# Dilated attention stage: sums read back at a written place, gate and first O loaded behind the last transposing transfer, the last pair's q scaled on VectorE

## The chip, the cores and the metric

The kernel runs on one core of a Trainium2 chip. The metric is device time in microseconds. A core has engines that each work through their own instructions in order: TensorE (PE, with PEld for its weight loads), VectorE (DVE), ScalarE (ACT), GpSimd (POOL) and SyncE (SP). SP issues most of the transfers, ACT some; the issues stand in the engine's order, so a transfer that must wait holds those behind it. Transfers issued by SP and ACT share eight semaphores in turn: an issue also waits until the transfer eight issues before it, on the same semaphore, has landed.

## The reference

Two layers on one sequence of 1024 positions, width 1024. Layer 0 uses latent attention, layer 1 dilated window attention; each layer ends with a squared-ReLU MLP. The change lies in layer 1's mixer:

```python
DIL_GROUPS = ((128, 1), (512, 4), (2048, 16))      # (window, dilation)

def dilated_mixer(h, pos, w_in, g_q, g_k, rel_bias, w_o):
    B, S, _ = h.shape
    proj = (h @ w_in).reshape(B, S, N_DIL_GROUPS, 3, DIL_HEADS, DIL_HEAD_DIM)
    outs, lses = [], []
    for gi, (window, dilation) in enumerate(DIL_GROUPS):
        q = rms_norm(proj[:, :, gi, 0], g_q[gi])
        k = rms_norm(proj[:, :, gi, 1], g_k[gi])
        v = proj[:, :, gi, 2]
        table = rel_bias[:, gi * DIL_HEADS:(gi + 1) * DIL_HEADS]
        o, lse = dilated_group(q, k, v, pos, table, window, dilation)
        outs.append(o)
        lses.append(lse)
    o_all = jnp.stack(outs, axis=0)
    wts = jax.nn.softmax(jnp.stack(lses, axis=0), axis=0)
    o = jnp.einsum('gbsh,gbshd->bshd', wts.astype(o_all.dtype), o_all)
    return o.reshape(B, S, DIL_HEADS * DIL_HEAD_DIM) @ w_o
```

`dilated_group` is softmax attention over the keys within the window, at multiples of the dilation, with a bias per head. Three groups of 16 heads of 64 are merged with weights from their softmax denominators, and the result goes through `w_o`.

## The kernel before, in words

The dilated stage (`dil`, from about 1535 to 2330 us) walks over 3 groups x 8 head pairs x 4 steps, in that order. Each step takes a quarter of the 1024 rows of one head pair: PE projects q and k in two halves of 24 matmuls (`psproj`), VectorE and GpSimd normalise them, PE transposes the rows into `kT` (`psq`, L2316), forms the scores of earlier rows (`pss`, L2345), and multiplies older probabilities with v (`psav`, L2424 and L2425). Numbers are split into a high and a low half-precision part (`ph` for probabilities, `kT`, `oT`), so a product takes three matmuls. In this half-precision form (`self.half` true) the kernel's normal run is made; a second form of the whole program stands behind a flag and does not run here.

`qkstep` ends with q and k scaled by their norms on VectorE (`qn`, L2305); q then takes its gain on GpSimd (L2307). `attend` makes the scores: VectorE adds the bias and takes the maximum (L2366), ACT exponentiates (`dnb` L2370, `pd` L2372), `ph` is split on ACT (L2409) and GpSimd or VectorE (L2410), and SP transposes it by a transfer, `pT<-ph` (L2411). For the steps after the last projection the transposition is made on PE instead (`pspt`, L2398).

Maxima and sums of all heads are kept in `stat`. Groups 0 and 1 hold their rows in another order than group 2, so what they leave goes through memory: each pair's output `U` (L2448, L2452), and, when the last pair of the group is done, the sums `S0` and `S1` (L2456, L2460). In group 2, `um` (issued by ACT) brings U of groups 0 and 1 back. `finish` of the first pair of group 2 reads the sums back (L2467), four transfers. `factors` turns them into merging weights on VectorE (`mgm` … `mgf`), and `merge` multiplies (`um` on GpSimd and U on VectorE, L2501; sums L2503) into one result per pair, which is transposed (`psot`) to O (`oT`) and, for pairs 0 to 5, put into memory (`oTd`).

The output projection behind the stage reads O back by `reload` (L1372, three double pairs of 512 rows, two transfers each) and multiplies with `wo` (`psy`); the raw weights come by the L538 transfers named `wor`. Its gate is a row of the conditioning broadcast to all partitions (L381, 512 KB). These loads are issued by `tail` in the last steps (`wor`, gate) and when the last step, `n == end`, has been issued (first O).

The order on SP, VectorE, ACT and GpSimd is decided by a scheduler from dependencies, priorities by program place, and a simulated timeline. PE's order is pinned as written up to `n == end` (`pin_from`), and scheduled after that. `pinned` keeps an instruction at its written place.

## Time and profile before

| what | value |
|---|---|
| median of 3 runs | 3006.09 us (3002.42 to 3009.18) |
| the profiled execution's own time | 3005.26 us |
| its span | 3003.1 us |
| mean granted PE clock | .985 |
| PE's longest waits of the dilated stage | 6.2, 5.8 and 4.4 us |

The span is what the profile covers; the times of the runs hold a little more. A row of the timeline gives start, duration, engine, line, operation, tiles written and read, and in brackets the idle time before it with what ended it. A row of the waits gives the total, the count and the longest wait in us.

### The profile page before, as it was taken

The page shows a single profiled execution, that of the slowest core. Times are in us where ns is not written, and L with a number is a line of the kernel's source. Part 1 is how long each engine was busy: PE and PEld are TensorE (multiplying, and loading weights), DVE is VectorE, ACT ScalarE, POOL GpSimd, SP SyncE. Part 2 cuts the span into 40 slices and gives each one's busy share as a digit, 9 for nine tenths or more (in the row PEclk, how much of TensorE's full clock was granted, in tenths as well). Part 3 has the DMA queues.
Part 4 walks back from the last instruction along what each step waited for, and adds up shares of the span by engine and source line. Part 5 has one row for each costly group of instructions (what it writes and reads, how often), then busy time and mean ns, then how long its engine had stood idle before and what let it go on. Part 6 is the DMA issues. An engine that isn't in the chain of part 4 may idle for free. (4 is left out here: it accounts for less than half of the span.)

```text
span 3003.1 us, 54490 instructions
## 1 busy us (share of the span) xinstructions
PE 2827.4 (94%) x20148; PEld 1676.0 (56%) x20148; DVE 2251.4 (75%) x4902; ACT 1684.2 (56%) x3491; POOL 922.6 (31%) x1276
## 2 busy tenths in 40 slices
PE   6878999999999999999999989998998989999998
PEld 5634566544444444444468878876875434444443
DVE  5687777658988966788768877776886699779565
ACT  4677888825455534533238777775664355555341
POOL 6578888700211000000123344453552002110010
PEclk9999999999999999999999999999999999999999
DMA  6267455425654799546436666565656555457763
GB/s 209 72 169 161 94 117 101 131 84 188 235 188 168 251 278 289 199 159 225 171 116 148 146 139 165 145 128 117 150 129 171 144 191 210 158 186 248 238 196 86
DMA packets 589680, 503.08 MB, mean 168 GB/s; under 512 B 292277, under 2 KB 482018, under 8 KB 589402
## 3 DMA queue, kind: packets, MB, share of 16 engines
q1 hardware_dynamic: 553722, 400.74, 47.9%
q0 software_dynamic: 25248, 87.22, 7.9%
q10 hardware_dynamic: 10432, 11.54, 1.6%
q8 instruction: 159, 2.61, 0.4%
q14 instruction: 119, 0.97, 0.1%
HBM read 317.40 MB, written 125.12 MB: 147 GB/s over the span
## 5 line engine op out<-in xcount | busy, mean ns | idle before, releaser
L534 PE MATMUL psm<-hf,wf 128*128 128x512 f16 x896 | 335.8, 381 | 11.1 <-DVE wf L161 11.1
L532 PE MATMUL psm<-hf,wf 128*128 128x512 f16 x896 | 341.0, 381 | 5.0 <-ACT wf L156 5.0
L533 PE MATMUL psm<-d,d 128*128 128x512 f16 x896 | 340.8, 381 | 4.7 <-DVE d L161 4.7
L534 PE MATMUL psm<-d,d 128*128 128x512 f16 x896 | 340.7, 380 | 0.0
L533 PE MATMUL psm<-hf,wf 128*128 128x512 f16 x896 | 340.6, 380 | 0.0
L532 PE MATMUL psm<-d,d 128*128 128x512 f16 x896 | 335.0, 380 | 0.3 <-ACT d L156 0.3
L1276 POOL TENSOR_TENSOR pp<-p,pp 128x1024 f16<-128x1024 f32 x125 | 275.4, 2209 | 57.9 <-ACT pp L1269 47.8
L532 PE MATMUL psproj<-wqk,hTp 128*128 128x256 f16 x1024 | 283.0, 276 | 0.0
L533 PE MATMUL psproj<-wqk,hTp 128*128 128x256 f16 x1024 | 282.3, 276 | 0.0
L534 PE MATMUL psproj<-wqk,hTp 128*128 128x256 f16 x1024 | 282.0, 275 | 0.0
L156 ACT ACTIVATE d<-ufr 128x1024 f16<-128x1024 f32 x112 | 117.8, 1052 | 211.3 <-PE psm L534 173.3
L897 DVE TENSOR_REDUCE mx<-pmx 128x1 f32<-128x512 f32 x240 | 162.8, 687 | 78.8 <-PE pmx L895 77.4
L161 DVE SCALAR_TENSOR_TENSOR d<-ufr,d 128x1024 f16<-128x1024 f32 x112 | 136.5, 1219 | 76.5 <-ACT d L156 76.4
L1268 ACT ACTIVATE p<-pss 128x512 f32<-128x512 f32 x256 | 149.9, 590 | 43.2 <-PE pss L1259 41.8
L2372 ACT ACTIVATE pd<-pd,dnb 128x192 f32<-128x192 f32 (+2 forms) x384 | 167.3, 437 | 4.1 <-POOL y L2301 2.3
L534 PEld LDWEIGHTS <-wf 128*128 128x128 f16 x896 | 87.8, 98 | 123.3 <-DVE wf L161 19.2
L532 PEld LDWEIGHTS <-wf 128*128 128x128 f16 x896 | 87.9, 98 | 112.9 <-ACT wf L156 10.9
L534 PEld LDWEIGHTS <-d 128*128 128x128 f16 x896 | 87.9, 98 | 111.0 <-issue 6.4
L532 PEld LDWEIGHTS <-d 128*128 128x128 f16 x896 | 88.0, 98 | 106.3 <-issue 2.2
L533 PEld LDWEIGHTS <-d 128*128 128x128 f16 x896 | 87.9, 98 | 106.4 <-issue 2.5
L2410 POOL TENSOR_TENSOR ph<-pd,ph 128x512 f16<-128x512 f32 (+1 forms) x121 | 113.3, 942 | 109.3 <-ACT ph L2409 109.1
L533 PEld LDWEIGHTS <-wf 128*128 128x128 f16 x896 | 88.0, 98 | 104.9 <-issue 1.8
(439 smaller groups left out, 8122.2 us busy)
## 6 DMA issues: line engine op xcount, KB each, us to landing
ufr<-uf SPq DMA_DIRECT2D x112, 512.0 KB
w2r<-in_mlp_w SPq DMA_DIRECT2D x96, 512.0 KB
adaw<-in_ada_w SPq DMA_DIRECT2D x80, 512.0 KB
w1r<-in_mlp_w SPq DMA_DIRECT2D x64, 512.0 KB
wqkr<-in_dil_w_in SPq DMA_DIRECT2D x96, 256.0 KB
wvr<-in_dil_w_in SPq DMA_DIRECT2D x34, 512.0 KB
uf<-ub POOLq DMA_DIRECT2D x32, 512.0 KB, 3.8
uf<-ua POOLq DMA_DIRECT2D x32, 512.0 KB, 3.3
```

The source lines that it names most:

```text
L156: nc.scalar.activation(hi, src, AF.Copy, scale=scale)
L161: return nc.vector.scalar_tensor_tensor(lo, src, scale, hi, op0=ALU.mult, op1=ALU.subtract, accum_out=self.seen[:, self.nseen - 1 : self.n ...
L532: mm(out, lh, rh, start=first, stop=False)
L533: mm(out, lh, rl, start=False, stop=False)
L534: mm(out, ll, rh, start=False, stop=last)
L897: nc.vector.tensor_reduce(maxes[h][:, 2 * j + b : 2 * j + b + 1], ps, op=ALU.max, axis=AX.X)
L1268: nc.scalar.activation(p[:, b * 512 : (b + 1) * 512], ps[b], AF.Exp, scale=1.0 / self.ss)
L1276: eng.tensor_tensor(q[:, 1], p, q[:, 0], op=ALU.subtract)
L2372: nc.scalar.activation(p[:, e, lo:hi], p[:, e, lo:hi], AF.Exp, scale=1.0 / self.ss, bias=nb[:, e : e + 1], accum_out=stat[:, g, t, 1, 2 * ...
L2410: (nc.gpsimd if i or u["g"] == 2 else nc.vector).tensor_tensor(lo, p, hi, op=ALU.subtract)
```

## The change

Four edits, all within the half-precision form. First, the read-back of the sums becomes a function, `sums_back(k)`, with pinned transfers: `S0` is read back when pair 2 of group 1 is finished, and `S1` when pair 0 of group 2 is, the place in the code where both were read before. Second, the gate's load leaves `tail` and becomes a callback, `back`. Third, `back` and the first O loads are issued one step later, when step `end + 1` has been written out. Fourth, the gain of q for the last pair of group 2 is multiplied on VectorE.

```diff
     def dil(self, at0, at1, tail, wqk, vd, back=None):
...
-            nc.gpsimd.tensor_tensor(qq, qq, gain[:, g : g + 1, :].unsqueeze(1).broadcast_to([P, 2, 2, 64]), op=ALU.mult)
+            (nc.vector if self.half and (g, u["pr"]) == (2, 7) else nc.gpsimd).tensor_tensor(qq, qq, gain[:, g : g + 1, :].unsqueeze(1).broadcast_to([P, 2, 2, 64]), op=ALU.mult)
...
+                if (g, pr) == (1, 2):
+                    sums_back(0)
                 return
 
             if pr == 0:
-                for k in range(2):
-                    v = Sd[k].rearrange("(l t r) e -> r l t e", t=8, r=2)
-                    for i in range(2):
-                        nc.sync.dma_start(out=stat[64 * i : 64 * i + 64, k].rearrange("p t k h -> p t (k h)"), in_=v[i])
+                sums_back(1)
...
+        def sums_back(k):
+
+            v = Sd[k].rearrange("(l t r) e -> r l t e", t=8, r=2)
+            for i in range(2):
+                self.pinned(nc.sync.dma_start(out=stat[64 * i : 64 * i + 64, k].rearrange("p t k h -> p t (k h)"), in_=v[i]))
...
-                    for pp in range(3):
-                        self.reload(O, src, pp, 0, nc.sync)
+                    if not self.half:
+                        for pp in range(3):
+                            self.reload(O, src, pp, 0, nc.sync)
+            if self.half and n == end + 1:
+                back()
+                for pp in range(3):
+                    self.reload(O, src, pp, 0, nc.sync)
...
+        def back():
+            got["gate"] = k.gate(1, 0)
+
...
             if tp == 3:
-                got["gate"] = k.gate(1, 0)
+                if not half:
+                    back()
```

On SP, where the sums of group 1 have just been written (`S`), before:

```order
L2460 DMA S_16274<-stat 512x1x32
L2467 DMA stat<-S_16274 64x8x32 x2
L2452 DMA U<-U_24430 512x1x128
L2411 DMA_TRANSPOSE pT_25491<-ph_25490 128x16x128
L2411 DMA_TRANSPOSE pT_25646<-ph_25645 128x8x128
L1968 DMA wqkr_25803<-in_dil_w_in 128x4x128
L2452 DMA U<-U_24430 512x1x128
```

and the same place now (weights of the projection are `wqkr`, the bias is `bt`):

```order
L2460 DMA S_16274<-stat 512x1x32
L2452 DMA U<-U_24432 512x1x128
L2411 DMA_TRANSPOSE pT_25493<-ph_25492 128x16x128
L2411 DMA_TRANSPOSE pT_25648<-ph_25647 128x8x128
L1968 DMA wqkr_25805<-in_dil_w_in 128x4x128
L2452 DMA U<-U_24432 512x1x128
L1968 DMA wqkr_25805<-in_dil_w_in 128x4x128
L2411 DMA_TRANSPOSE pT_25785<-ph_25784 128x8x128
L2354 DMA bt_26745<-bias_139 128x2x128
L2411 DMA_TRANSPOSE pT_25912<-ph_25911 128x8x128
L1968 DMA wqkr_26070<-in_dil_w_in 128x4x128
L2479 DMA stat<-S_16274 64x8x32 x2
```

The two read-backs have gone from right behind the write of `S` to behind four more transposes, and stand between two weight loads.

On SP at the end of the stage, before:

```order
L538 DMA wor_29204<-in_dil_w_o 128x2x512
L381 DMA gate_29465<-gates 128x1024
L538 DMA wor_29467<-in_dil_w_o 128x2x512
L2411 DMA_TRANSPOSE pT_29128<-ph_29127 128x8x128
L538 DMA wor_29472<-in_dil_w_o 128x2x512
L1372 DMA oT_29536<-oTd 128x2x512 x2
L1372 DMA oT_29539<-oTd 128x2x512 x2
L1372 DMA oT_29542<-oTd 128x2x512
L2411 DMA_TRANSPOSE pT_29252<-ph_29251 128x8x128
L1372 DMA oT_29542<-oTd 128x2x512
L2411 DMA_TRANSPOSE pT_29383<-ph_29382 128x8x128
L1372 DMA oT_29786<-oTd 128x2x512 x2
```

and now:

```order
L538 DMA wor_29204<-in_dil_w_o 128x2x512
L538 DMA wor_29465<-in_dil_w_o 128x2x512
L2411 DMA_TRANSPOSE pT_29128<-ph_29127 128x8x128
L538 DMA wor_29470<-in_dil_w_o 128x2x512
L2411 DMA_TRANSPOSE pT_29252<-ph_29251 128x8x128
L2411 DMA_TRANSPOSE pT_29383<-ph_29382 128x8x128
L381 DMA gate_29607<-gates 128x1024
L1372 DMA oT_29609<-oTd 128x2x512 x2
L1372 DMA oT_29612<-oTd 128x2x512 x2
L1372 DMA oT_29615<-oTd 128x2x512 x2
L1372 DMA oT_29786<-oTd 128x2x512 x2
```

The last three transposes now stand ahead of the gate and all of O.

On PE behind the last projection, from the last matmul of the scores on, before:

```order
L2345 MATMUL pss_29546<-kT_28967 128x256
L532 LDWEIGHTS oT_29536
L532 MATMUL psy_29849<-wo_29334,oT_29536 128x512
L533 LDWEIGHTS oT_29536
L533 MATMUL psy_29849<-wo_29334,oT_29536 128x512
L534 LDWEIGHTS oT_29536
```

and now:

```order
L2345 MATMUL pss_29535<-kT_28967 128x256
L2398 MATMUL pspt_29549<-ident,pd_29550 128x128
L2316 MATMUL psq_29570<-ident,qn_29365 128x128 x4
L2525 MATMUL psot_29581<-ident,U_28418 128x128 x4
L2525 MATMUL psot_29588<-ident,U_28418 128x128 x4
L2398 MATMUL pspt_29549<-ident,pd_29550 128x128
L2398 MATMUL pspt_29549<-ident,pd_29559 128x128 x2
```

Before, 22 `psy` matmuls of the output projection stood between these scores and the first `pspt`. Now the transpositions follow directly, and the first `psy` comes behind the next scores.

## The prediction

> **What bounds the kernel now.** I read the page first, then PE's waits in the dilated stage, then three of those waits up their queues.

> ```profile
> PE 2827.4 (94%) x20148; PEld 1676.0 (56%) x20148; DVE 2251.4 (75%) x4902; ACT 1684.2 (56%) x3491; POOL 922.6 (31%) x1276
> PE psav L2424 <- DMA pT<-ph: 21.0, 9, 6.2
> PE psq L2316 <- POOL qn L2307: 5.8, 1, 5.8
> ```

> PE is busy 94% of the span, so the change is worth only the PE idle time that it removes, and what follows from it. The last two rows are those of PE's waits from 1770 to 2420 us (total, count, longest) that the diff touches. Three single waits are longer than 4 us, and each has a second price:

> ```profile
> 2060.00:2080.00 20.00, 13.77 (x117) 11.13 (x115) 7.00 (x28) 8.02 (x31) 5.61 (x12) 0.83 0.73 161
> 2260.00:2280.00 20.00, 14.84 (x143) 12.12 (x141) 10.91 (x39) 11.78 (x36) 4.69 (x8) 0.94 1.10 262
> 2280.00:2300.00 20.00, 13.67 (x90) 8.98 (x89) 15.29 (x39) 5.35 (x19) 9.66 (x18) 0.81 0.62 153
> 2070.38 0.29 PE L2424 MATMUL psav<-vs,pT 128*128 128x128 f16 x1 [6.23 <-DMA pT<-ph]
> 2073.56 0.42 PE L534 MATMUL psproj<-wqk,hTp 128*128 128x256 f16 x1
> 2076.35 0.27 PE L533 MATMUL psproj<-wqk,hTp 128*128 128x256 f16 x1
> ```

> In the windows the numbers are the busy time of PE, PEld, DVE, ACT and POOL, then the granted clock, the DMA share and GB/s. PE loses most, and the clock falls to .83, .94 and .81, in just the windows with the long waits. After the 6.23 us wait a projection matmul lasts .42 us until 2276, then .27 again: about 2.6 us of the next step go to the half clock. Short waits (2.94 us, below) show no such fall. [...]

> **Sums of group 1 read back (stall A).**

> ```profile
> 2056.32 0.56 SPq L2460 DMA_DIRECT2D S<-stat  x1
> 2062.71 1.21 SPq L2467 DMA_DIRECT2D stat<-S  x2
> 2064.01 0.58 SPq L2452 DMA_DIRECT2D U<-U  x1
> 2064.70 4.93 SPq L2411 DMA_TRANSPOSE pT<-ph  x2
> SPq L2467 <- DMA S<-stat: 5.7, 1, 5.7
> 2057.77 1.58 POOL L2410 TENSOR_TENSOR ph<-pd,ph 128x256 f16<-128x256 f32 x2 [1.01 <-ACT ph L2409]
> 2058.11 0.75 DVE L2432 TENSOR_REDUCE U<-psav 128x128 f32<-128x256 f32 x2
> ```

> SP works strictly in order. It stands 5.7 us until the sums written at 2056.32 have landed, then issues two read-backs, the write of U, and only then the transpose whose `ph` was complete at 2059.35 (2057.77 + 1.58). PE wanted that transpose at 2070.38 − 6.23 = 2064.15. Without the read-backs the U write goes out when its reduce is done, 2058.86 (2058.11 + .75). From the U issue to `psav` it was 2070.38 − 2064.01 = 6.37 us; kept, `psav` starts at 2065.2, or 1.1 us late. The rings were still busy with loads issued just before, so I add .7: 1.8 remains of 6.23. Gone: 4.4 us and the half clock behind it, 2.65: **7.1 us** (6.2 if 2.7 us remain; 8.9 if nothing does).

> The read-backs now stand two transposes later, ahead of a weight load; their two issues (1.21 us) fall in SP's free time, and the factors on VectorE (`mgm`) that need them stand later in its order too, behind the next steps' q work. I cost that at nothing; if a factor waits there for the read, the q work queued behind it on VectorE waits, and PE with it, one for one.

> **Sums of group 0 (stall A').**

> ```profile
> SPq L2467 <- DMA S<-stat: 2.2, 1, 2.2
> 1807.39 1.93 SPq L2411 DMA_TRANSPOSE pT<-ph  x1
> 1811.62 0.23 PE L2424 MATMUL psav<-vs,pT 128*128 128x128 f16 x1 [2.94 <-DMA pT<-ph]
> 1870.85 0.23 PE L2424 MATMUL psav<-vs,pT 128*128 128x128 f16 x1 [1.26 <-DMA pT<-ph]
> ```

> The same pattern, 2.94 us. The transpose could be issued 2.8 us earlier (2.2 waited, and one of two issues in 1.21), but it stands behind the same loads of v as its sister of the next pair of pairs, which still left 1.26 us at 1870.85. I take 1.6 left, so **1.3 us** gained (bounds 0 and 2.9). The new place, behind the U write of pair 2, costs two issues, 1.1 us, which the next transposes have in hand.

> **Gate and first O (stall B), q of the last pair (stall C).**

> ```profile
> SPq L381 <- DMA um<-U: 4.4, 1, 4.4
> 2264.66 0.34 SPq L381 DMA_DIRECT2D gate<-gates  x1
> 2266.64 0.37 SPq L538 DMA_DIRECT2D wor<-in_dil_w_o  x1
> 2268.69 1.84 SPq L2411 DMA_TRANSPOSE pT<-ph  x1
> 2277.57 0.29 PE L2424 MATMUL psav<-vs,pT 128*128 128x128 f16 x1 [4.36 <-DMA pT<-ph]
> 2289.82 0.69 PE L2316 MATMUL psq<-ident,qn 128*128 128x128 f32 x2 [5.83 <-POOL qn L2307]
> 2285.97 2.49 POOL L2501 TENSOR_TENSOR um<-um,mgf 128x512 f32<-128x512 f32 x2
> 2282.75 0.68 DVE L2305 TENSOR_TENSOR qn<-psproj,dry 128x512 f32<-128x512 f32 x1
> 2283.35 1.15 DVE L2501 TENSOR_TENSOR U<-U,mgf 128x512 f32<-128x512 f32 x1
> 2296.65 0.68 DVE L2501 TENSOR_TENSOR U<-U,mgf 128x512 f32<-128x512 f32 x1
> ```

> B: the gate load waited 4.4 us for its DMA slot. In the new order a `wor` load takes that slot and its wait, so only the gate's own issue, one slot, and its 512 KB ahead of the transpose go. The transpose moves up to the second `wor`'s place, 2266.64 against 2268.69, 2.1 us, and its packets pass the gate's: I estimate 3.3 us, `psav` at 2274.3. It then wants kT, which ACT makes behind a weight conversion that now stands earlier; I put the end of this projection half at 2279.4.

> C: `qn` is ready on VectorE at 2283.43 (2282.75 + .68), but GpSimd scales it only after four `um` products, the last two of which end at 2288.46, and PE's 5.83 us are spent on that. On VectorE the scaling stands behind one product U·mgf: .68 us alone, 1.15 beside a busy GpSimd. The scaling of 128x256 elements has no VectorE row: .35 (half of the .68 of a 128x512 one) to 1.3 (a GpSimd product's length, if it must wait one out); I take .5, nearest to the .68 row. [...]

> With B's advance `qn` is done at about 2280.8 and `psq` starts at 2282.6 instead of 2289.82: PE still waits 3.2 us there. Now to what is next:

> ```profile
> 2295.45 0.83 PE L2345 MATMUL pss<-kT 64*128 64x256 f16 x12
> 2296.21 0.39 PE L532 MATMUL psy<-wo,oT 128*128 128x512 f16 x1
> 2300.75 0.38 PE L532 MATMUL psy<-wo,oT 128*128 128x512 f16 x1
> 2296.06 0.68 DVE L2296 TENSOR_REDUCE dms<-dsq 128x8 f32<-128x512 f32 x1
> 2300.25 0.28 DVE L2366 CUSTOM_DVE_ANT_0 pd<-pss,bt 128x128 f32<-128x128 f32 x1
> 2301.94 1.48 PE L2398 MATMUL pspt<-ident,pd 128*128 128x128 f32 x4 [0.81 <-ACT pd L2372]
> 2323.03 0.33 PE L2398 MATMUL pspt<-ident,pd 128*128 128x128 f32 x1 [1.74 <-ACT pd L2372]
> ```

> The scores end at 2296.21, and `pspt` can start only at 2301.94, since VectorE works through `dms` … `qn` from 2296.06 before it reaches them at 2300.25. Before, 22 `psy` matmuls (2296.21 to 2300.75) fill that gap. They need the first O. With its loads behind the last transpose, the order puts all `psy` behind `pspt`, `psq`, `psot` and the next scores: the 5.7 us become PE idle time, some 6.5 with two scalings (.5 each) more on VectorE.

> Sum for the end: from `psq` to the end of these scores it was 6.4 us, an estimated 2.2 of them by the half clock; 4.2 kept, they end at 2286.8 instead of 2296.21, 9.4 us earlier; then 6.5 us idle, `pspt` at about 2293.3. Before, at 2301.94, 22 `psy` of .216 us were done, which is the same as having been there at 2297.2: 3.9 us gained, less about 1.3 for a half clock behind the new idle time and a wait for kT, plus 1.74 − .7, since the third chain at 2323.03 gets more cover and the second less. **3.6 us** (−3 to +9).

> Total 7.1 + 1.3 + 3.6 = 12.0. The profiled execution took 3005.26 (span 3003.1), .83 under the median 3006.09; from the median I forecast 2994.1. About 6 us (0.2%) is what a measurement here can tell from no change.

> **Rivals.**

> *All stalls vanish.* The transposes land in time and the uncovered chain runs without its VectorE queue: 8.9 + 2.9 + 9 = 20.8, so 2985. For it: the queue's 5.7 us are the plain cause of A. Against: 1.26 us is left at 1870.85, and `dms` to scores is plain work.

> *The uncovered chain eats the end, and A keeps half.* The half clock stays on from the 3.2 us wait through the 6.5 us one, which costs about 2.6 us for a projection half and 1.5 for the rest: the end is −1. The transposes still stand behind the loads, A gives 5 and A' 0: together 4, so 3002.

> *The moves do nothing.* If U's write, not the read-back, holds the transpose, A stays: only 4.9 us, 3001. It shares its chance with the last.

> *Slower: the first O comes late.* Its loads stand behind the last transpose, which waits for GpSimd's `ph` behind four `um` products.

> ```profile
> 2290.42 1.23 SPq L2411 DMA_TRANSPOSE pT<-ph  x1
> 2291.75 3.09 SPq L1372 DMA_DIRECT2D oT<-oTd  x6
> SPq L538 <- DMA um<-U: 13.6, 1, 13.6
> ```

> Before, that transpose left at 2290.42. The `um` products can start with the factors, near 2280.2; four of 1.25 and two of `ph` put it near 2287.5, the loads to 2293, the first pair landed near 2296, before `psy` wants it at 2298. Each us later costs one. It decides from 2310: no gain; 2316 is 0.2% slower. Possible if an O load inherits the slot that held the `wor` loads for 13.6 us behind a read of U; in the new order only the last load of the second half does, and its matmuls come after 2330. With the issue at 2316 and some 2 us to land, the end would be 8 us later than before: 3014.

> **How the numbers follow.** Forecast .53 (2988 to 2999), all vanish .10, chain or nothing .29, slower .08. The range takes in the first three: 2985 to 3003.5. Faster by over 0.2%: the first two and a little of the third, .67; within 0.2% .25; slower .08.

> **What will show it.** Right, if `psav` near 2065 waits under 3 us with the clock at 1.00 from 2060 to 2080; if `psq` near 2283 waits about 3 us on VectorE; if `pspt` afterwards waits 5 to 7 us for ACT. Wrong, if `psav` still waits for SP, if `mgm` waits for the read-backs, or if `psy` waits for a DMA of O.

## The result and the profile after

| | before | change |
|---|---|---|
| median of 8 runs | 3004.49 us | 2995.98 us |
| lowest to highest | 3002.42 to 3010.56 | 2991.36 to 2998.11 |
| profiled execution, its span | 3005.26, 3003.1 | 2996.41, 2994.6 |
| mean granted clock of the span | .985 | .983 |

The ratio of the change to before is .9966, with a 95% interval of .9955 to .9977. That is about 10 us by the ratio and 8.5 by the medians. The forecast was 2994.1, a gain of 12.0 from 3006.09. The total came out as forecast, but the profile shows that it is not made of the forecast's terms.

PE's waits of the changed kernel from 1770 to 2420 us come first (total, count, longest):

```profile
PE psav L2424 <- DMA pT<-ph: 11.2, 7, 4.1
PE pss L2345 <- DVE qn L2305: 5.8, 1, 5.8
PE psot L2525 <- DVE U L2508: 4.3, 2, 2.3
```

The waits for transposed probabilities went from 21.0 us to 11.2, and the 5.8 us of `psq` for GpSimd's q have become .50 for VectorE's (below). Two rows are new: `pss` on `qn` (5.8) and `psot` on the merged U (4.3). Next, four windows of the same kernel (busy time of PE, PEld, DVE, ACT and POOL, then the granted clock):

```profile
2050.00:2070.00 20.00, 18.28 (x194) 15.72 (x192) 13.11 (x48) 14.49 (x54) 8.65 (x17) 1.00 1.12 222
2085.00:2105.00 20.00, 15.66 (x131) 12.74 (x128) 16.15 (x49) 10.63 (x37) 12.73 (x18) 0.83 0.49 107
2260.00:2280.00 20.00, 14.47 (x114) 10.63 (x115) 14.68 (x44) 11.48 (x36) 7.30 (x9) 0.83 0.70 166
2280.00:2300.00 20.00, 11.23 (x88) 8.72 (x86) 16.72 (x54) 7.06 (x23) 5.05 (x11) 0.74 0.63 198
```

and single PE instructions of it, with the idle time before them and its releaser in brackets:

```profile
1812.25 0.22 PE L2424 MATMUL psav<-vs,pT 128*128 128x128 f16 x1
2062.94 0.23 PE L2424 MATMUL psav<-vs,pT 128*128 128x128 f16 x1 [1.09 <-DMA pT<-ph]
2093.28 0.63 PE L2525 MATMUL psot<-ident,U 128*128 128x128 f32 x4 [2.28 <-DVE U L2508]
2095.96 1.09 PE L2525 MATMUL psot<-ident,U 128*128 128x128 f32 x4 [2.06 <-DVE U L2508]
2270.51 0.23 PE L2424 MATMUL psav<-vs,pT 128*128 128x128 f16 x1 [3.12 <-DMA pT<-ph]
2279.59 0.44 PE L2316 MATMUL psq<-ident,qn 128*128 128x128 f32 x2 [0.50 <-DVE qn L2307]
2288.99 1.46 PE L2345 MATMUL pss<-kT 64*128 64x256 f16 x11 [5.80 <-DVE qn L2305]
2291.98 0.48 PE L2398 MATMUL pspt<-ident,pd 128*128 128x128 f32 x1 [1.53 <-ACT pd L2372]
```

Stall A (6.23 us) is down to 1.09 and stall A' (2.94) is gone. The dip of the clock at 2070 is gone too, but a new dip to .83 stands at 2085 to 2105, with the two `psot` waits, and a deeper one (.74) at 2280 to 2300, with the 5.80 and 1.53 us. At 2260 to 2280 the clock was .94 before and is .83 now: behind the shorter `psav` wait (3.12 us against 4.36) the half clock lasts 6.83 us against 3.41.

Where the 8.5 us of span went is read from the starts of the same matmuls in both traces. The tile views give the last ones; each row ends with the first and last start and the form. Before:

```profile
L2425 PE MATMUL psav<-vs,pT x640: 192/193/261, 1564.8 to 2327.7; 128*128 128x64 f16 x160
L534 PE MATMUL psy<-wo,oT x256: 377/379/380, 597.9 to 2395.0; 128*128 128x512 f16 x128
L534 PE MATMUL psm<-d,d x896: 377/379/634, 992.7 to 2992.2; 128*128 128x512 f16 x180
```

and of the change:

```profile
L2425 PE MATMUL psav<-vs,pT x640: 192/193/261, 1564.7 to 2322.5; 128*128 128x64 f16 x160
L534 PE MATMUL psy<-wo,oT x256: 377/379/390, 598.8 to 2390.6; 128*128 128x512 f16 x128
L534 PE MATMUL psm<-d,d x896: 377/379/631, 992.3 to 2983.7; 128*128 128x512 f16 x180
```

The lead is 5.2 us at the end of the stage's `psav`, 4.4 at the end of the output projection and 8.5 at the last MLP matmul. So **half of the lead arises behind everything that the change touches**: the MLP takes 597.2 us before (2992.2 − 2395.0) and 593.1 now. The same subtraction, for stretches between numbered matmuls, gives a table for all kernels that were run. Each entry is that kernel's stretch minus the stretch of before, in one profiled execution of each:

| kernel | start to ~1788 | to ~2050 (A') | to ~2190 (A) | to ~2264 | to last `psav` (end) | to last `psy` | MLP |
|---|---|---|---|---|---|---|---|
| change | +2.3 | −4.6 | −3.8 | 0 | +.9 | +.8 | −4.1 |
| change again | +.7 | −2.6 | −2.4 | +1.7 | +2.9 | +.8 | −4.1 |
| s1_mid | +1.3 | −3.8 | −4.8 | 0 | +.1 | +.8 | −4.1 |
| undo_sums | +1.6 | +2.6 | −.5 | 0 | +.3 | +.8 | −4.1 |
| s0_only | +5.0 | −3.9 | −.7 | 0 | +2.3 | +.8 | −4.1 |
| undo_q | −.5 | −4.0 | −2.3 | +1.7 | +6.9 | +.8 | −4.1 |
| gate_o | +2.6 | +1.0 | −1.0 | 0 | +5.4 | +.8 | −4.1 |
| q_only | +1.3 | +1.5 | −.4 | 0 | −1.3 | −.6 | −.4 |
| sums_q | +3.3 | −2.0 | −3.4 | +1.7 | +1.6 | 0 | −.5 |
| mid_sums_q | +1.0 | −.3 | −2.4 | +1.7 | −.9 | −.6 | −.5 |
| o_early | +2.1 | −2.2 | −4.2 | 0 | −1.2 | +.1 | −4.1 |
| mid_o_early | +1.1 | −2.9 | −4.1 | 0 | −1.9 | −.6 | −1.7 |
| wor_late_p | +2.7 | −2.2 | −3.9 | +1.7 | −10.9 | −.1 | −1.7 |

The first column stands ahead of everything that the edits move, so it says how far single executions wander: −.5 to +5.0. The 0 or +1.7 of the column to 2264 is the same kind of thing, one half clock more or less. The last column hardly wanders; it takes one of three values.

### The profile page after: what moved, and what is told of

It is laid out like the page before. It is cut to its first block, busy times and chain, and to the rows that moved or that the text cites. A ratio compares the mean times of both kernels' runs of the same rounds, so it can differ in the third digit from the quotient of the medians.

```text
span 2994.6 us, 54486 instructions
## 1 busy us (share of the span) xinstructions
PE 2829.0 (94%) x20148; PEld 1679.2 (56%) x20148; DVE 2252.4 (75%) x4906; ACT 1685.8 (56%) x3491; POOL 922.5 (31%) x1272
## 5 line engine op out<-in xcount | busy, mean ns | idle before, releaser
L532 PE MATMUL psm<-hf,wf 128*128 128x512 f16 x896 | 340.3, 380 | 5.4 <-ACT wf L156 5.4
L533 PE MATMUL psm<-d,d 128*128 128x512 f16 x896 | 340.2, 380 | 4.7 <-DVE d L161 4.7
L534 PE MATMUL psm<-hf,wf 128*128 128x512 f16 x896 | 334.7, 380 | 7.9 <-DVE wf L161 7.9
L534 PE MATMUL psm<-d,d 128*128 128x512 f16 x896 | 340.2, 380 | 0.0
L533 PE MATMUL psm<-hf,wf 128*128 128x512 f16 x896 | 340.1, 380 | 0.0
L532 PE MATMUL psm<-d,d 128*128 128x512 f16 x896 | 334.7, 380 | 0.3 <-ACT d L156 0.3
L532 PE MATMUL psproj<-wqk,hTp 128*128 128x256 f16 x1024 | 283.3, 277 | 0.0
L533 PE MATMUL psproj<-wqk,hTp 128*128 128x256 f16 x1024 | 282.9, 276 | 0.0
L534 PE MATMUL psproj<-wqk,hTp 128*128 128x256 f16 x1024 | 282.6, 276 | 0.0
L2372 ACT ACTIVATE pd<-pd,dnb 128x192 f32<-128x192 f32 (+2 forms) x384 | 167.3, 437 | 4.8 <-POOL y L2301 1.7
L534 PEld LDWEIGHTS <-wf 128*128 128x128 f16 x896 | 87.7, 98 | 118.5 <-DVE wf L161 13.9
L532 PEld LDWEIGHTS <-wf 128*128 128x128 f16 x896 | 87.8, 98 | 113.3 <-ACT wf L156 10.8
L534 PEld LDWEIGHTS <-d 128*128 128x128 f16 x896 | 87.8, 98 | 110.7 <-issue 5.9
L2410 POOL TENSOR_TENSOR ph<-pd,ph 128x512 f16<-128x512 f32 (+1 forms) x121 | 114.0, 948 | 113.2 <-ACT ph L2409 112.8
L533 PEld LDWEIGHTS <-d 128*128 128x128 f16 x896 | 87.8, 98 | 106.2 <-issue 2.0
L532 PEld LDWEIGHTS <-d 128*128 128x128 f16 x896 | 87.9, 98 | 106.0 <-issue 1.7
L533 PEld LDWEIGHTS <-wf 128*128 128x128 f16 x896 | 87.8, 98 | 104.3 <-issue 0.8
```

What stands on the lines that cost most here:

```text
L532: mm(out, lh, rh, start=first, stop=False)
L533: mm(out, lh, rl, start=False, stop=False)
L534: mm(out, ll, rh, start=False, stop=last)
L2372: nc.scalar.activation(p[:, e, lo:hi], p[:, e, lo:hi], AF.Exp, scale=1.0 / self.ss, bias=nb[:, e : e + 1], accum_out=stat[:, g, t, 1, 2 * ...
L2410: (nc.gpsimd if i or u["g"] == 2 else nc.vector).tensor_tensor(lo, p, hi, op=ALU.subtract)
```

## The experiments

Twelve kernels, timed in three groups beside the kernel before (its medians in the groups: 3006.72, 3008.11, 3008.46). Each diff is against the changed kernel unless it says otherwise.

| kernel | group | median us | ratio to before, 95% interval |
|---|---|---|---|
| s1_mid | 1 | 2995.21 | .9967 (.9955 to .9979) |
| o_early | 1 | 2996.96 | .9972 (.9960 to .9983) |
| undo_sums | 1 | 3002.98 | .9988 (.9979 to .9996) |
| undo_q | 1 | 3003.12 | .9988 (.9980 to .9997) |
| mid_o_early | 2 | 2996.15 | .9963 (.9950 to .9976) |
| sums_q | 2 | 3002.51 | .9984 (.9974 to .9995) |
| gate_o | 2 | 3011.18 | 1.0007 (.9998 to 1.0016) |
| s0_only | 2 | 3000.10 | .9978 (.9968 to .9987) |
| change again | 3 | 2999.60 | .9969 (.9957 to .9981) |
| q_only | 3 | 3005.51 | .9989 (.9980 to .9998) |
| mid_sums_q | 3 | 2997.48 | .9960 (.9946 to .9974) |
| wor_late_p | 3 | 2988.05 | .9933 (.9920 to .9947) |

### Where the gain of stall A went: S1 read back earlier (s1_mid)

```diff
+            if (g, pr, t) == (2, 0, 5):
+                sums_back(1)
             if t == 7:
                 finish(u)
...
-            if pr == 0:
-                sums_back(1)
```

> The change, with the sums of group 1 read back one step and a half earlier (behind the second U write of the last pair of group 1, where SP has nothing to issue for 6 us) and all else as changed. Theory 'late factors': in the changed kernel the factors of pair 0 of group 2 come late on VectorE because their read-back is written late, and psot waits 2.3 + 2.1 us for the merged U with a half clock of 6.83 us behind it. Here mgm returns to its old place in VectorE's order, both waits and the half clock go, -6 to -7 us: about 2989. Rival 'the merge is late anyway' (GpSimd's um products set it): psot still waits 3 us or more, 2995 to 2997. Rival 'the read-back blocks SP again': psav at about 2063 waits 5 us again, 2999 or more. In this version the last psproj and the second pss behind it also lie in different PSUM banks (6 and 7), in the changed kernel in the same one (7): if that is what held pss for 5.8 us, that wait is gone here and pspt waits in its place.

In the change SP issues the read-back of S1 four transposes behind the write of S1:

```profile
2054.02 0.56 SPq L2460 DMA_DIRECT2D S<-stat  x1
2056.58 0.55 SPq L2452 DMA_DIRECT2D U<-U  x1
2057.23 6.02 SPq L2411 DMA_TRANSPOSE pT<-ph  x2
...
2070.85 1.25 SPq L2411 DMA_TRANSPOSE pT<-ph  x1
...
2076.68 1.23 SPq L2411 DMA_TRANSPOSE pT<-ph  x1
...
2078.60 1.26 SPq L2479 DMA_DIRECT2D stat<-S  x2
```

So the first maximum that needs it (`mgm`) and all merging behind it stand later on VectorE. `mgm` did not wait for the read-back: both halves had landed by 2081.87, and VectorE had no idle time between there and `mgm`. The same kernel's VectorE:

```profile
2083.62 0.22 DVE L2490 TENSOR_REDUCE mgm<-stat 128x16 f32<-128x48 f32 x1
2088.10 2.14 DVE L2506 TENSOR_TENSOR U<-U,mgf 128x512 f32<-128x512 f32 x2
2092.21 2.37 DVE L2508 TENSOR_TENSOR U<-U,um 128x512 f32<-128x512 f32 x2
```

Before, `mgm` started at 2082.87, when PE was some 10 us less far: against before, PE's `psproj` of the change have a lead of 2.3 us at 2061, 10.1 at 2082 and 12.3 at 2097 (times of the kernel before). Then `psot`, at its old place in PE's order, waits 2.28 and 2.06 us for the last sums of U, the clock halves for 6.83 us, and the lead is 5.6 at 2112. So 6.7 of the 10 us that were won there are given back within 15 us.

With the read-back two transposes earlier no `psot` waits, but PE's scores wait in their place, as they did before. In s1_mid:

```profile
2086.27 0.28 PE L2345 MATMUL pss<-kT 64*128 64x256 f16 x2 [1.61 <-ACT kT L2321]
2088.20 0.72 PE L2345 MATMUL pss<-kT 64*128 64x256 f16 x10 [1.66 <-DVE kT L2322]
```

What follows: the late read-back does cause the `psot` waits, which are gone here. But the 6 to 7 us that were expected of this did not come: the stretch is 1.0 us shorter (−4.8 against −3.8), and the timing can't tell the two apart (.9967 against .9966). Our reading is that the merging work has to be done in these 20 us in either order, so that who waits for it changes and the sum hardly does: from 2080 to 2100 us VectorE is busy for 19.89 us in the change and for 17.55 in s1_mid. That VectorE is the limit was not tried by itself.

### What each half of the sums is worth (undo_sums, s0_only)

undo_sums puts both read-backs where they were; s0_only puts back that of S1 alone, so that S0 stays at its new place. The diff of undo_sums:

```diff
-                if (g, pr) == (1, 2):
-                    sums_back(0)
...
-                sums_back(1)
+                for k in range(2):
+                    v = Sd[k].rearrange("(l t r) e -> r l t e", t=8, r=2)
+                    for i in range(2):
+                        nc.sync.dma_start(out=stat[64 * i : 64 * i + 64, k].rearrange("p t k h -> p t (k h)"), in_=v[i])
```

> The change with the sums of both groups read back as before (gate, O and q stay changed). Theory: stalls A' (2.9 us) and A (6.2 us with 2.6 to 4 us of half clock) return, the two psot waits (4.3 us and their half clock, 2.4) go: +5 to +6 us, 3001 to 3002. Rival 'A is the whole gain': psot's waits have another cause and stay, +10 or more, 3006. Rival 'no part': 2996.

and of s0_only:

```diff
-                sums_back(1)
+                v = Sd[1].rearrange("(l t r) e -> r l t e", t=8, r=2)
+                for i in range(2):
+                    nc.sync.dma_start(out=stat[64 * i : 64 * i + 64, 1].rearrange("p t k h -> p t (k h)"), in_=v[i])
```

> The change with only the sums of group 1 read back as before; those of group 0 stay at the new place. Against undo_sums (both as before, ratio 0.9988) it shows the sums of group 0 alone, against the change those of group 1 alone. Theory: stall A' (1.9 us in undo_sums) goes, A stays with 6.1 us and its half clock, psot does not wait: -2 to -3 us against undo_sums, ratio 0.9978 to 0.9982. Rival 'the loads of v hold that transpose': no difference from undo_sums.

The rows of PE's waits are from 2060 to 2110 us, of undo_sums:

```profile
PE psav L2424 <- DMA pT<-ph: 6.1, 1, 6.1
```

and of s0_only:

```profile
PE psav L2424 <- DMA pT<-ph: 6.2, 1, 6.2
```

Stall A is back in both, with its length of before, and `psot` waits in neither. From 1800 to 1815 undo_sums has a wait of 1.9 us for `pT` and s0_only none, so each wait hangs on its own read-back. Both times came as expected or within a microsecond of it. In time, S0 alone is worth .0010 (.9988 to .9978), about 3 us, and S1 on top of it .0012 (.9978 to .9966), 3.6 us. The intervals of neighbouring kernels overlap, so each of these steps is a size and not a proof. For both together (.0022) the intervals of undo_sums and the change lie apart, if barely (from .9979, up to .9977; up to .9981 for change again). The table agrees in its means: in the column A' the ten rows with S0 moved have −2.9 and the three without +1.7, a difference of 4.6; in the column A the nine with S1 moved have −3.5 and the four without −.7, a difference of 2.8.

### The three other edits, one by one (undo_q, gate_o, q_only, sums_q)

undo_q puts only the scaling back on GpSimd. gate_o is undo_sums and undo_q together, so it has the gate and the first O moved and nothing else. q_only is the kernel before with the scaling moved, the first diff's removed line in the place of its added one. sums_q has gate and O where they were. The diff of undo_q:

```diff
-            (nc.vector if self.half and (g, u["pr"]) == (2, 7) else nc.gpsimd).tensor_tensor(qq, qq, gain[:, g : g + 1, :].unsqueeze(1).broadcast_to([P, 2, 2, 64]), op=ALU.mult)
+            nc.gpsimd.tensor_tensor(qq, qq, gain[:, g : g + 1, :].unsqueeze(1).broadcast_to([P, 2, 2, 64]), op=ALU.mult)
```

and that of sums_q:

```diff
-                    if not self.half:
-                        for pp in range(3):
-                            self.reload(O, src, pp, 0, nc.sync)
-            if self.half and n == end + 1:
-                back()
-                for pp in range(3):
-                    self.reload(O, src, pp, 0, nc.sync)
+                    for pp in range(3):
+                        self.reload(O, src, pp, 0, nc.sync)
...
-                if not half:
-                    back()
+                back()
```

> The change with q of the last pair scaled on GpSimd again (sums, gate and O stay changed). Theory: the scaling stands behind four um products and two ph there, psq starts near 2284.5 instead of 2279.6, +4 to +5 us: about 3000. Rival 'VectorE's queue sets it anyway' (the gap behind pss is set by U merges and q norms on VectorE, which scaling on GpSimd relieves by three products): 0 to +1 us, 2996 to 2997.

> Only the second and third edit (gate and first O behind the last transpose); sums and q as before. Theory: stall B shrinks from 4.4 to 3.2 us and C from 5.8 to about 3.9 (q starts earlier), but the gap behind the scores opens to 7 us and halves the clock: 0 to +3 us, ratio 1.000 to 1.001. Rival: the order alone is worth it, -3 us or more, 0.999 or less.

> The kernel before with the fourth edit alone (q of the last pair scaled on VectorE). Last psproj and second pss lie in different banks here. Theory: stall C (5.8 us and 6.8 us of half clock, some 8 us together) goes, while psy still covers the gap; VectorE's later products take 1 to 3 back: -4 to -6 us, ratio 0.998 to 0.9987. Rival 'q needs the other edits' (VectorE is as late as GpSimd when the wor, gate and O loads stand ahead): within 2 us of before, 0.9993 or more.

> The change without its second and third edit: gate and first O are loaded where they were before; sums moved and q on VectorE as changed. Theory 'gate and O give nothing net': psav waits 4.4 instead of 3.1 us, but psy covers the gap behind the scores again as far as the bank allows: within 2 us of the change, ratio 0.9960 to 0.9973. Rival 'the move is worth stall B': the 4.4 us and the lost advance of q come back, +5 us: 0.998 or more.

PE's waits from 2255 to 2330 us in gate_o:

```profile
PE pspt L2398 <- ACT pd L2372: 5.7, 1, 5.7
PE psq L2316 <- POOL qn L2307: 4.1, 1, 4.1
PE psav L2424 <- DMA pT<-ph: 2.8, 1, 2.8
```

and in q_only:

```profile
PE pspt L2398 <- ACT pd L2372: 4.6, 2, 2.9
PE psav L2424 <- DMA pT<-ph: 4.6, 1, 4.6
PE psq L2316 <- DVE qn L2307: 1.7, 1, 1.7
```

The scaling on VectorE alone removes most of stall C and gives 3.3 us (.9989), a little less than expected. Gate and O alone shorten the wait of stall B from 4.36 to 2.8 us, uncover `pspt` (5.7), and give no gain, as expected: 1.0007 (.9998 to 1.0016), and that with the MLP 4.1 us shorter. Without the scaling (undo_q) the change loses two thirds of its gain, .9988 (3003.12 us, where about 3000 was expected). Without gate and O (sums_q) it has .9984, which was forecast for the case that moving them is worth stall B. But the sums alone, by the steps above, would be near .9978 and the scaling would add .0011, so .9967. The parts do not add up, and the next kernels show one reason.

### The cover of the uncovered chain (o_early, mid_o_early, mid_sums_q)

o_early puts the first O's loads back to `n == end` and keeps the gate late; mid_o_early is that and s1_mid; mid_sums_q is sums_q and s1_mid. The diff of o_early:

```diff
-                    if not self.half:
-                        for pp in range(3):
-                            self.reload(O, src, pp, 0, nc.sync)
+                    for pp in range(3):
+                        self.reload(O, src, pp, 0, nc.sync)
             if self.half and n == end + 1:
                 back()
-                for pp in range(3):
-                    self.reload(O, src, pp, 0, nc.sync)
```

> The change with only the gate behind the last transposing transfer; the first O loads stand ahead of the last two transposes again, as before. Theory 'cover lost': the 22 psy matmuls again fill the gap between the scores and pspt, -4 to -6 us: 2990 to 2992. Rival 'bank': the second pss stands in the same PSUM bank (7) as the last psproj, so pss itself waits for qn on VectorE and the psy behind it can start only after that wait; the cover returns too late to hide more than the 1.5 us in front of pspt, -1 to -2 us: 2994 to 2995, pss still waiting 5 to 6 us. Rival 'O delays the transposes': psav behind the last transposes waits for a DMA again, slower than the change.

> The change with both: sums of group 1 read back one step and a half earlier, and the first O loads ahead of the last two transposes again (gate behind them, q on VectorE). Here the last psproj and the second pss lie in different PSUM banks, so the psy matmuls can start right behind the scores. Theory 'cover lost': the 7.5 us that pspt waited in s1_mid shrink to 2 or 3, with no half clock behind them, -5 to -6 us against s1_mid: ratio to before 0.9945 to 0.9955. Rival 'VectorE sets the end': the psy moved into the gap leave other gaps open behind them (psq, third chain), -1 to -2 us: 0.996 to 0.9965. Rival 'O delays the transposes': psav waits again, above 0.997.

> sums_q (gate and O loaded as before, sums moved, q on VectorE) with the sums of group 1 read back one step and a half earlier, as in s1_mid. What differs at the end of the stage is the PSUM bank of the last psproj: 6, not 7, so the second pss need not wait for it. Theory 'bank': the 6.4 us that pss waited in sums_q become a wait of pspt of 1 to 3 us under the cover of psy, -3 to -4 us against sums_q (0.9984): 0.9971 to 0.9976. Rival 'VectorE sets it whatever the bank': the same wait moves to pspt or psq and the ratio stays at 0.998 or above.

The same place behind the last projection, first in s1_mid (no `psy` ahead of `pspt`):

```profile
2290.09 0.48 PE L2398 MATMUL pspt<-ident,pd 128*128 128x128 f32 x1 [7.52 <-ACT pd L2372]
```

then in o_early:

```profile
2290.14 1.46 PE L2345 MATMUL pss<-kT 64*128 64x256 f16 x11 [5.79 <-DVE qn L2305]
```

then in mid_o_early:

```profile
2291.32 1.63 PE L2398 MATMUL pspt<-ident,pd 128*128 128x128 f32 x4 [2.66 <-ACT pd L2372]
```

then in sums_q:

```profile
2296.08 1.46 PE L2345 MATMUL pss<-kT 64*128 64x256 f16 x11 [6.38 <-DVE qn L2305]
```

and in mid_sums_q:

```profile
2298.49 1.24 PE L2398 MATMUL pspt<-ident,pd 128*128 128x128 f32 x3 [2.87 <-ACT pd L2372]
```

A bank is one of the buffers that the kernel's pools hand out for the results of matmuls, here numbered 0 to 7. In the change, o_early and sums_q it is the second bank of these scores that waits, and the releaser is the `qn` that reads the last `psproj`, which the scores themselves do not read. In the built programs that bank is the one that the last `psproj` holds (bank 7); in s1_mid, mid_o_early and mid_sums_q the last `psproj` holds bank 6. These bank numbers are read from the programs; no trace shows them. The traces show where the wait stands: in the change, its repetition, o_early, undo_q and sums_q, which are all those that read S1 back at the late place, `pss` waits 4.2 to 6.4 us for `qn`; in the nine others it does not. Where nothing covers the chain this only moves the wait: 5.80 and 1.53 in the change, 7.52 in s1_mid. Where 22 `psy` stand behind the scores, the scores must not wait, or the cover comes too late: 2.66 against 5.79, 2.87 against 6.38.

Timed, sums_q with the bank free goes from .9984 to .9960, more than expected (their intervals touch at .9974), and its end of stage from +1.6 to −.9 (−1.3 in q_only, where `pss` does not wait either). So moving the sums late had cost the scaling its cover. But o_early (expected at 2990 to 2992) and mid_o_early (expected at .9945 to .9955) both missed the gain of the regained cover, and do not differ by more than their intervals (.9972, .9963), nor mid_o_early from the change. That the wait of `pss` comes with the late S1 is shown; its price in time is not settled (2.7 to 7.2 us by the two pairs of ratios).

### A version that keeps the cover (wor_late_p)

s1_mid, and: first O loaded one step earlier than in the kernel before and held at that place (`reload` takes the holding function as an argument); the last two `wor` loads moved from `tail` to behind the last transposes.

```diff
+            if self.half and n == end - 1:
+                for pp in range(3):
+                    self.reload(O, src, pp, 0, nc.sync, self.pinned)
             if self.half and n == end + 1:
                 back()
-                for pp in range(3):
-                    self.reload(O, src, pp, 0, nc.sync)
...
         def back():
+            wo[0].extend(k.wo_load(a["dil_w_o"][0], 0, dp) for dp in range(2, 4))
             got["gate"] = k.gate(1, 0)
...
-                wo[0].extend(k.wo_load(a["dil_w_o"][0], 0, dp) for dp in range(2, 4))
```

> A version made from what the runs showed: sums of group 1 read back one step and a half earlier; the first O loads pinned between the last two transposes, where SP has nothing to issue; the last two wor loads moved behind the last transpose together with the gate, so that neither their packets nor their two conversions (1.06 us on ACT and 1.22 on VectorE each) stand ahead of the last scores; q on VectorE. Theory: psav behind the third last transpose waits 1 to 2 us in place of 3.1 and no half clock follows it, psq does not wait, pspt waits under 3 us under psy: -4 to -7 us against mid_o_early (0.9963): 0.994 to 0.995. Rival: the late wor loads make psy wait for wo (psy pairs 2 and 3 need them) or the end of the stage is bound by VectorE's merges all the same: 0.996 or more.

> The change itself once more, beside the runs of this call. Ratio 0.9955 to 0.9977 as before, psav near 2063 waiting about 1 us, psot 2.3 and 2.1 us, pss and pspt behind the last projection some 7 us together.

SP's queue in wor_late_p:

```profile
2266.86 6.32 SPq L2411 DMA_TRANSPOSE pT<-ph  x2
2273.28 3.09 SPq L1372 DMA_DIRECT2D oT<-oTd  x6
2282.27 1.23 SPq L2411 DMA_TRANSPOSE pT<-ph  x1
2283.60 0.53 SPq L538 DMA_DIRECT2D wor<-in_dil_w_o  x1
```

PE's waits from 2255 to 2330 us in the same kernel:

```profile
PE pspt L2398 <- ACT pd L2372: 3.3, 2, 2.6
...
PE psy L532 <- ACT wo L156: 0.4, 1, 0.4
```

and two windows of it:

```profile
2260.00:2280.00 20.00, 17.96 (x187) 15.60 (x187) 16.74 (x52) 13.35 (x48) 11.52 (x18) 1.00 0.83 213
2280.00:2300.00 20.00, 16.78 (x96) 8.92 (x95) 13.79 (x47) 6.80 (x24) 2.31 (x4) 0.91 0.69 195
```

Between 2255 and 2330 us no `psav` and no `psq` waits any more, the clock stays at 1.00 to 2280, `psy` covers the chain and hardly waits for the late weights. The end of the stage is 10.9 us shorter than before. Timed it is .9933 (.9920 to .9947), better than the .994 to .995 expected: 20 us under the kernel before and 11.6 under the change in the same group (2988.05 against 2999.60), the intervals of the two ratios apart. The change itself came back at .9969, as expected.

## Why the prediction was right, and where it was not

**The total: right, for partly other reasons.** 2994.1 forecast, 2995.98 measured, within the range. By the profile the change has four terms: A' about −3 to −4.6, A about −3, the end of the stage +.9 to +2.9 and the way to the last `psy` +.8, the MLP −4.1. The prediction had −1.3, −7.1, −3.6 and nothing. So the good number is luck in part: up to the last `psy` the profiled execution has a lead of 4.4 us, not 12, and the MLP, which the forecast does not count, brought 4.1 more. The median of before, 3004.49 now, also lies 1.6 under the 3006.09 that the forecast started from.

Of the three signs named for "right", only the first came: `psav` near 2063 waited 1.09 us with the clock at 1.00. `psq` waited .50 and not about 3, and `pspt` 1.53 and not 5 to 7, since `pss` had waited 5.80 ahead of it. Of the signs for "wrong" none came: SP no longer stood ahead of the transpose of stall A, `mgm` did not wait for the read-backs, nor `psy` for O.

**Stall A: the term was right at its own place, and lost next door.** The wait fell to 1.09 us (1.8 forecast) and the half clock vanished. PE's lead grew by 7.8 us from 2061 to 2082, against 7.1. The step that failed is "I cost that at nothing": the factors do stand later on VectorE, and the price was the one the prediction named, PE waiting one for one, though through `psot` and not through q. 6.7 us went back; of 7.1 some 3 stayed. The read-backs were also said to stand "two transposes later"; the order quoted ahead of the prediction shows four. s1_mid, where it is two, kept only a microsecond more.

**Stall A': right mechanism, wrong size.** 1.3 us was taken because a sister transpose behind the same loads still left 1.26. Nothing was left: the `psav` at 1812.25 does not wait. The term measured about 3 us by time and 4.6 in the table's means, at or over its upper bound of 2.9. A row from another pair was taken as a floor, and it was not one.

**Stall B: the wrong cause.** The transpose was to move up from 2268.69 to the place of the second `wor`, 2266.64. But it stood where it did for another reason: GpSimd had just finished the `ph` that it reads, at 2268.66 (2267.26 + 1.40). Before:

```profile
2267.26 1.40 POOL L2410 TENSOR_TENSOR ph<-pd,ph 128x256 f16<-128x256 f32 x1 [1.06 <-ACT ph L2409]
```

and the transpose in the change:

```profile
2262.87 1.23 SPq L2411 DMA_TRANSPOSE pT<-ph  x1
```

It leaves 5.82 us earlier in time, again .03 us behind its `ph` (ready at 2262.84), and that is no more than the lead of 6.1 us which the kernel already had at 2264. What did change is how long the transfer takes: from its issue to its landing 8.8 us before, 7.6 in the change, 7.0 in o_early and 3.2 in wor_late_p, against 2.7 for the next transpose of the change, issued at 2275.02. So the gate ahead of it cost about 1.2 us, and in wor_late_p, where the last two `wor` loads stand behind it as well, the wait is gone. That the bytes of these loads are what slows the transfer is our reading; it was not tried apart from the order.

From `psav` to the end of its projection half it was 6.4 us before; the prediction put down 5.1, as if no half clock came, and 8.6 came (2270.51 to 2279.09), with the clock at half for 6.83 us. So at that point a gain of 4.6 us was forecast (2279.4 against 2283.99), and 1.2 were lost (2279.09, less the lead of 6.1).

The slot that the gate waited for is in the trace of before. SP and ACT issue 1114 transfers on eight semaphores, 139 or 140 on each, and 1069 of the 1113 steps from one issue to the next in time go to the next semaphore. The gate's load is on that of the `um` issued at 2258.44, whose last landing there is at 2264.59; the gate was issued at 2264.66.

**Stall C: right, and by more.** 3.2 us of wait was forecast on VectorE's `qn`, .50 remained, in part because PE itself came later than forecast. From 2283.99 to `psq` at 2289.82 were 5.83 us; 2.6 of them were to be gained, and 5.3 were. The scaling took:

```profile
2278.27 1.26 DVE L2307 TENSOR_TENSOR qn<-qn,dgain 128x256 f32<-128x256 f32 x1
2285.66 0.42 DVE L2307 TENSOR_TENSOR qn<-qn,dgain 128x256 f32<-128x256 f32 x1
```

So .42 without GpSimd and 1.26 beside its `um` (2.49 us for two, from 2276.76). The prediction took .5, and 1.3 at most, if a GpSimd product must be waited out. The 1.26 is about the length of one `um` (1.25), and the .42 was measured with GpSimd idle (from 2284.62 to 2288.29). What slows the scaling beside `um` the traces do not show.

**The uncovered chain: right in kind, short in size.** 6.5 us of idle time was forecast where `psy` had stood; 5.80 + 1.53 = 7.33 came, though most of it in front of `pss` and not in front of `pspt`. From `psq` to `pspt` it took 12.4 us (2279.59 to 2291.98), against 10.7 forecast (2282.6 to 2293.3). With B short by 5.8 us, C better by 2.7 and this longer by 1.7, the end came out at a small loss instead of −3.6; "the uncovered chain eats the end" (−1) was the better account of this stretch.

**Not in the sum: the MLP.** PE's waits from 2395 to 2440 us, before:

```profile
PE psm L532 <- ACT wf L156: 2.1, 2, 1.1
PE psm L534 <- DVE wf L161: 2.0, 1, 2.0
```

and in the change:

```profile
PE psm L532 <- ACT wf L156: 3.0, 2, 2.7
```

The scheduler orders the conversions of the MLP's first weights otherwise once the gate comes late, and two waits (2.70 and .26 us) take the place of three. Eight of the ten executions with the gate late show 593.0 us for the MLP, mid_o_early and wor_late_p 595.4, and the three with the gate at its old place 596.7. The step follows from the gate's place: o_early and sums_q differ in that alone, with −4.1 against −.5. It arises in the first 71 us: at the matmul that started at 2465.91 before, both executions of the change have the whole 4.1. That the new order of conversions is the means is read from the waits and was not tried by itself, and these waits explain only about 1 of the 4 us. The rest stays open.

**The rival "slower, O comes late"** did not happen: the O loads left at 2285.74 to 2300 and the first `psy` at 2298.48 did not wait for them. "The moves do nothing" is excluded by undo_sums and s0_only, where the stalls come back with the read-backs.

## What to carry to other kernels

A stall removed on an in-order queue is a gain only until the next thing that the moved instruction feeds: follow the moved transfer through its consumer's whole queue to the next engine that waits, over the next 30 us, before costing it at nothing (6.7 of 10 us went back here). Before a transfer is moved up, look at when its data was complete: an instruction that leaves right behind its data gains nothing from an earlier place (the transpose of stall B left .03 us behind its `ph`). Work that fills a gap (here 22 `psy`) can be worth as much as the stall that is removed at its cost (gate_o uncovered 5.7 us and gained nothing), so move the loads that stand in the transfer's way (`wor`, gate) and keep those that feed the filler. And a scheduler decides anew everything behind an edit: compare the stretches that the edit doesn't touch, too, before a total is taken as proof of its terms.

## What the runs showed of the hardware that was not expected

The prediction held that waits as short as 2.94 us cost no clock. The trace that it read shows otherwise in two places: in the kernel before, the clock halves with a wait of 2.36 us (from 1755.27, for 3.41 us) and with one of 2.71 us (from 2011.27, for 6.83 us). In the change it halves for 6.83 us, from 2094.07, with the waits of 2.28 and 2.06 us that stand .6 us of work apart. Two other waits, of 2.77 us near 1786 and 2.62 near 2038, halve it in the change and not before, which may be one source of the 2 to 5 us by which single profiles wander.
